# State-space products split between VectorE and GpSimd, results placed three steps behind

## The chip, the cores and the metric

The kernel runs on one core of a Trainium2 chip. The core has five engines, each with its own queue of instructions, executed in order: TensorE (PE in the profile; PEld is its weight load), VectorE (DVE), ScalarE (ACT), GpSimd (POOL) and SyncE (SP, which here only issues DMAs). The metric is the device time of one execution in microseconds, the median of several runs.

## The reference, cut to what matters

Two small networks run one behind the other on the same activations of 256 tokens and 1024 features, all in float32. The first has two layers, each with a token mixer and a feed-forward part with a short convolution. The second has two layers too; its first mixer contains a state-space part (S5) with complex diagonal states. Before that part can run, its parameters have to be discretised:

```python
dt = exp(log_dt); mag = exp(a_re * dt)
abar_re, abar_im = mag * cos(a_im * dt), mag * sin(a_im * dt)
coef_re = (xr * ar + xi * ai) / den;  coef_im = (xi * ar - xr * ai) / den   # xr = abar_re - 1, xi = abar_im
bb_re = coef_re * br - coef_im * bi
bb_im = coef_re * bi + coef_im * br
...
s[t] = abar * s[t-1] + bb @ u[t]            # complex, per group and state
y = s_re @ c_re.T - s_im @ c_im.T + d * u
```

The kernel handles four tokens at a time. So it needs `bb`, `abar * bb`, `abar^2 * bb`, `abar^3 * bb`, and likewise `c` times `abar` to the powers one to four: eight complex products in two chains of four.

## The kernel before, in words

Activations lie with features on the 128 partitions and tokens along the free dimension. Every weight matrix is streamed from memory in pieces of 1024 columns (`Piece`). Each piece is split into a high and a low part so that three fast matmuls replace one float32 matmul: ACT casts the high part (`whi`, L170), DVE subtracts it to get the low part (`wlo`, L172), and PE runs the three matmuls of `mm3` (L187, L188, L189). Four buffers each hold raw pieces, high parts and low parts.

A feed-forward part (`ffn`) has 22 chunks. Each chunk is two pieces, 16 groups of three matmuls, and then a tail: DVE scales the result (`ag`, L526), ACT and DVE do the convolution (`cv`, L531 and twice L539), ACT applies the activation (L541), POOL multiplies by the gate (`cv`, L542), ACT casts the high part (`ah`, L543), and POOL subtracts for the low part (`al`, L544).

The S5 preparation is a generator, `S5.prepare`. It runs as `side` work in the feed-forward part of the last layer of the first network: after each chunk, one or two `next(side)` trace a further stretch of it. `tc.issue_after` orders the POOL instructions of such a stretch behind that chunk's `al` on POOL, and orders nothing on other engines. A `yield` ends a stretch; each half (real or imaginary) of a complex product is one stretch.

A half is three POOL instructions on 128x256 elements (L728, L729, L730), with `tm` as scratch, whose tag differs for the two halves. The result is passed to `place`, which keeps a list `late`. When the list is longer than one, the oldest result is placed: two ACT activations (L721) copy it, masked by `half`, into the two 16-column sides of the padded matrices `B`, `C` or `C0` (the profile calls them s5b, s5c and E). The products alternate between two buffers in `pk` (s5pk), and read both halves of the product before. Sixteen halves follow one another: four products for `B` in one chain, four for `C` in another, in the same two buffers. Behind them stand small matmuls (L757), an ACT copy (L760), 32 transposes (L767) with ACT copies (L768), and the table of rotations (`turn`) on POOL.

The order of instructions on each engine is not the program's. The kernel is built with an automatic scheduler that orders the instructions of each queue by simulated times, with the program's order as priority, and inserts the waits. Inside one queue nothing can overtake at run time.

Of the kernel before, what the change touches and what calls it, by code (L numbers as in the profile page):

```python
# [14 lines left out]
ALU = mybir.AluOpType  # L15
# [83 lines left out]
def build(tc, A, O, stop=None):  # L99
    nc = tc.nc  # L100
    es = ExitStack()
    pool = lambda **k: es.enter_context(tc.tile_pool(**k))
    with es:
# [530 lines left out]
        class S5:  # L634
# [23 lines left out]
            def prepare(self, lbp):  # L658
# [6 lines left out]
                G2, GS = nc.gpsimd.tensor_tensor, nc.gpsimd.tensor_scalar  # L665
# [43 lines left out]
                x = lambda c: c.unsqueeze(2).to_broadcast([128, 16, 16])  # L709
                late = []  # L710

                def place(dst, v):

                    late.append((dst, v))
                    if len(late) > 1:
                        placed()

                def placed():
                    dst, v = late.pop(0)
                    for g in range(2):  # L720
                        nc.scalar.activation(dst[:, :, 16 * g:16 * g + 16], v, AF.Copy, scale=self.half[:, g:g + 1])  # L721

                def times(dst, o, a, re, im, ops=(ALU.subtract, ALU.add)):

                    for c, op in enumerate(ops):
                        tm = sp.tile([128, 512], F32, tag="t%d" % c, name="tm", bufs=1)[:, :256] \
                            .rearrange("p (a b) -> p a b", a=16)
                        G2(o[c], a[c], x(re), op=ALU.mult)  # L728
                        G2(tm, a[1 - c], x(im), op=ALU.mult)  # L729
                        G2(o[c], o[c], tm, op=op)  # L730
                        place(dst[c], o[c])
                        yield

                two_ = lambda t: [t[:, 0], t[:, 1]]
                b = [[B[:, c, :, j, :] for c in range(2)] for j in range(4)]
                at, to = two_(pk[:, 0]), two_(pk[:, 1])
                yield from times(b[3], to, at, cr, ci)
                for j in (2, 1, 0):
                    at, to = to, at
                    yield from times(b[j], to, at, are, aim)  # L740
                at, to = two_(Cp), two_(pk[:, 1])
                for c in range(2):
                    place(C0[:, c], at[c])
                for j in range(4):
                    yield from times(two_(C[:, j]), to, at, are, aim, (ALU.add, ALU.subtract))
                    at, to = to, (two_(pk[:, 0]) if j == 0 else at)
# [567 lines left out]
```

## Time and profile before

| what | value |
|---|---|
| median of 3 runs | 1554.58 us (1554.15 to 1555.01) |
| the profiled execution's own time | 1554.38 us |
| its span, first to last instruction | 1552.4 us |
| PE busy | 1516.7 us, 98% of the span |
| DVE, ACT, POOL busy | 1049.8, 794.9, 585.8 us |
| mean granted clock of PE | 0.992 |

The span lies inside the execution's own time; 2 us of start and end are around it. PE's busy time comes from modelled ends of pipelined matmuls, so its share tells less than the number of matmuls in a stretch of known length. The granted clock is a share of full speed.

### The profile page before, as it was taken

Reading aid. Unit: us, or ns where it says so; the run is one execution under the profiler, and the core shown is the slowest. Engines: PE = TensorE matmul, PEld = TensorE weight load, DVE = VectorE, ACT = ScalarE, POOL = GpSimd, SP = SyncE. Lnnn points to the kernel's source line nnn. Section 1 sums busy time; section 2 is a strip of 40 time slices with the busy share of each in tenths; the row PEclk is TensorE's granted clock in tenths of the full one; section 3 lists DMA queues with packets and bytes.
Section 4 is the critical chain, followed back from the end, with each engine's and each line's share of the span. In section 5 each row is a group of like instructions: output and inputs, shape, how many; then the busy total and the mean of one; then the engine's idle time right before and its main releaser. Section 6 shows DMA issues by size and latency. Waiting matters only on the chain.

```text
span 1552.4 us, 31045 instructions
## 1 busy us (share of the span) xinstructions
PE 1516.7 (98%) x12596; PEld 1479.0 (95%) x12596; DVE 1049.8 (68%) x1384; ACT 794.9 (51%) x1228; POOL 585.8 (38%) x610
## 2 busy tenths in 40 slices
PE   9999999999999999999989999999999998999997
PEld 8899999999999999999988999999999997999997
DVE  6856566877666666657567587888676667677654
ACT  4644444555444544445565644456555446565542
POOL 6500023433326000124998694435333312333332
PEclk9999999999999999999999999999999999999998
DMA  8554355555465644565444464335554554355553
GB/s 260 186 183 148 122 179 189 190 178 182 150 207 169 213 167 136 145 198 179 159 136 150 136 191 165 122 110 197 187 181 155 181 170 140 109 191 183 168 166 109
DMA packets 86574, 259.55 MB, mean 167 GB/s; under 512 B 13592, under 2 KB 24744, under 8 KB 86432
## 3 DMA queue, kind: packets, MB, share of 16 engines
q1 hardware_dynamic: 78688, 254.05, 50.5%
q10 hardware_dynamic: 7584, 3.21, 0.8%
q8 instruction: 98, 1.61, 0.4%
q0 software_dynamic: 160, 0.32, 0.1%
q14 instruction: 44, 0.36, 0.1%
HBM read 255.92 MB, written 1.10 MB: 166 GB/s over the span
## 4 chain that ended last, share of the span: by engine, by line
PE 80%; POOL 8%; DVE 7%; issue 2%; ACT 2%; DMA 1%; DVEq 0%; ACTq 0%; POOLq 0%
PE ps_mm L187 25%; PE ps_mm L188 25%; PE ps_mm L189 25%; DVE wlo L172 3%; POOL s5pk L730 1%; DVE xl L247 1%; POOL al L544 1%; PE ps_sm L443 1%; POOL tm L729 1%; POOL s5pk L728 1%; ACT whi L170 1%; DVE h L474 1%; PE ps_mm L1108 1%; POOL sq L259 0%; POOL cv L542 0%
## 5 line engine op out<-in xcount | busy, mean ns | idle before, releaser
L172 DVE TENSOR_TENSOR wlo<-raw,whi 128x1024 fp32r<-128x1024 f32 (+3 forms) x536 | 638.1, 1205 | 279.8 <-ACT whi L170 270.8
L170 ACT CAST whi<-raw 128x1024 fp32r<-128x1024 f32 (+3 forms) x536 | 510.2, 957 | 428.6 <-PE ps_mm L188 352.9
L189 PE MATMUL ps_mm<-xh,wlo 128*128 128x256 f32 x2352 | 670.8, 285 | 9.4 <-DVE wlo L172 9.2
L187 PE MATMUL ps_mm<-xh,whi 128*128 128x256 f32 x2352 | 669.4, 285 | 3.7 <-ACT whi L170 1.9
L188 PE MATMUL ps_mm<-xl,whi 128*128 128x256 f32 x2352 | 669.6, 285 | 1.7 <-DVE xl L247 1.7
L189 PEld LDWEIGHTS ps_mm<-xh,wlo 128*128 128x128 f32 x2352 | 453.1, 193 | 12.7 <-DVE wlo L172 12.7
L187 PEld LDWEIGHTS ps_mm<-xh,whi 128*128 128x128 f32 x2352 | 453.3, 193 | 5.2 <-ACT whi L170 4.9
L188 PEld LDWEIGHTS ps_mm<-xl,whi 128*128 128x128 f32 x2352 | 453.1, 193 | 4.3 <-DVE xl L247 4.2
L187 PE MATMUL ps_mm<-ah,whi 128*128 128x256 f32 x704 | 199.4, 283 | 0.0
L189 PE MATMUL ps_mm<-ah,wlo 128*128 128x256 f32 x704 | 199.3, 283 | 0.0
L188 PE MATMUL ps_mm<-al,whi 128*128 128x256 f32 x704 | 199.3, 283 | 0.0
L542 POOL TENSOR_TENSOR cv<-cv,ag 128x256 f32<-128x256 f32 x88 | 109.2, 1241 | 222.4 <-ACT cv L541 202.0
L259 POOL TENSOR_TENSOR sq<-h 128x256 f32<-128x256 f32 (+1 forms) x47 | 68.2, 1450 | 179.2 <-DVE h L567 88.0
L188 PEld LDWEIGHTS ps_mm<-al,whi 128*128 128x128 f32 x704 | 135.2, 192 | 0.0
L189 PEld LDWEIGHTS ps_mm<-ah,wlo 128*128 128x128 f32 x704 | 135.2, 192 | 0.0
L187 PEld LDWEIGHTS ps_mm<-ah,whi 128*128 128x128 f32 x704 | 135.2, 192 | 0.0
L539 DVE SCALAR_TENSOR_TENSOR cv<-ag,vec,cv 128x255 f32<-128x255 f32 (+1 forms) x176 | 95.9, 545 | 17.2 <-ACT cv L531 14.2
L465 POOL TENSOR_TENSOR gate<-gate 128x256 f32<-128x256 f32 x16 | 19.4, 1225 | 203.1 <-DVE gate L464 203.1
L544 POOL TENSOR_TENSOR al<-cv,ah 128x256 fp32r<-128x256 f32 x88 | 73.8, 838 | 45.8 <-ACT ah L543 45.8
L543 ACT CAST ah<-cv 128x256 fp32r<-128x256 f32 x88 | 35.7, 406 | 103.1 <-POOL cv L542 103.1
L526 DVE TENSOR_TENSOR ag<-ps_mm,rb 128x512 f32<-128x512 f32 x88 | 60.4, 687 | 38.5 <-PE ps_mm L189 38.1
L262 POOL TENSOR_TENSOR acc<-acc,sq 128x256 f32<-128x256 f32 x57 | 58.2, 1022 | 3.9
(343 smaller groups left out, 2120.4 us busy)
## 6 DMA issues: line engine op xcount, KB each, us to landing
raw<-w_up SPq DMA_DIRECT2D x88, 512.0 KB, 3.7
raw<-w_fi SPq DMA_DIRECT2D x88, 512.0 KB, 4.0
raw<-w_qk SPq DMA_DIRECT2D x48, 512.0 KB, 3.7
raw<-w_gate SPq DMA_DIRECT2D x32, 512.0 KB, 3.6
raw<-w_down SPq DMA_DIRECT2D x32, 512.0 KB, 3.6
raw<-w_fo SPq DMA_DIRECT2D x32, 512.0 KB, 3.6
raw<-w_v SPq DMA_DIRECT2D x24, 512.0 KB, 4.3
raw<-w_u SPq DMA_DIRECT2D x16, 512.0 KB, 6.2
```

Source lines behind the costliest of these rows:

```text
L170: nc.scalar.copy(self.hi[:, :n], raw[:, :n])
L172: eng.tensor_tensor(self.lo[:, :n], raw[:, :n], self.hi[:, :n].bitcast(F32), op=ALU.subtract)
L187: nc.tensor.matmul(out, lhsT=a[0], rhs=b[0], start=start, stop=False)
L188: nc.tensor.matmul(out, lhsT=a[0], rhs=b[1], start=False, stop=False)
L189: nc.tensor.matmul(out, lhsT=a[1], rhs=b[0], start=False, stop=stop)
L259: nc.gpsimd.tensor_tensor(q, hs, hs, op=ALU.mult)
L262: nc.gpsimd.tensor_tensor(acc, acc if k0 + i > 1 or n == 1 else q[:, 0, :], q[:, i, :], op=ALU.add)
L526: nc.vector.tensor_tensor(ag, ps, bc2(rb), op=ALU.mult)
L539: nc.vector.scalar_tensor_tensor(out=c[:, o], in0=a[:, s_], scalar=w[j], in1=c[:, o], op0=ALU.mult, op1=ALU.add)
L542: nc.gpsimd.tensor_tensor(c, c, ag[:, 1, :], op=ALU.mult)
L543: nc.scalar.copy(ah[:, i, :], c)
L544: last = nc.gpsimd.tensor_tensor(al[:, i, :], c, ah[:, i, :].bitcast(F32), op=ALU.subtract)
```

## The change

`G2`, which was `nc.gpsimd.tensor_tensor`, is replaced in `times` by an engine that goes with the half: the real half (c = 0) runs on VectorE, the imaginary half (c = 1) stays on GpSimd. All three instructions of a half go to one engine. The list of results waiting to be placed may now hold three.

```diff
                     late.append((dst, v))
-                    if len(late) > 1:
+                    if len(late) > 3:
                         placed()
...
                     for c, op in enumerate(ops):
                         tm = sp.tile([128, 512], F32, tag="t%d" % c, name="tm", bufs=1)[:, :256] \
                             .rearrange("p (a b) -> p a b", a=16)
-                        G2(o[c], a[c], x(re), op=ALU.mult)
-                        G2(tm, a[1 - c], x(im), op=ALU.mult)
-                        G2(o[c], o[c], tm, op=op)
+                        G = (nc.vector, nc.gpsimd)[c].tensor_tensor
+                        G(o[c], a[c], x(re), op=ALU.mult)
+                        G(tm, a[1 - c], x(im), op=ALU.mult)
+                        G(o[c], o[c], tm, op=op)
                         place(dst[c], o[c])
                         yield
```

`placed` and everything before and behind the products are unchanged. What remains in the list at the end is placed by the `while late` loop, as before.

## Rows read from the trace of the kernel before

**Rows 1.** The page: busy time by engine, and the last chain by line.
```profile
PE 1516.7 (98%) x12596; PEld 1479.0 (95%) x12596; DVE 1049.8 (68%) x1384; ACT 794.9 (51%) x1228; POOL 585.8 (38%) x610
...
PE ps_mm L187 25%; PE ps_mm L188 25%; PE ps_mm L189 25%; DVE wlo L172 3%; POOL s5pk L730 1%; DVE xl L247 1%; POOL al L544 1%; PE ps_sm L443 1%; POOL tm L729 1%; POOL s5pk L728 1%; ACT whi L170 1%; DVE h L474 1%; PE ps_mm L1108 1%; POOL sq L259 0%; POOL cv L542 0%
```

**Rows 2.** Stretches: length, busy PE, PEld, DVE, ACT, POOL, clock, DMA share, GB/s.
```profile
680.00:700.00 20.00, 20.00 (x169) 20.00 (x168) 10.85 (x12) 8.93 (x12) 5.91 (x5) 1.00 0.63 197
780.09:853.87 73.78, 65.10 (x610) 61.68 (x609) 50.24 (x50) 44.00 (x80) 65.82 (x70) 0.98 0.43 144
853.87:865.00 11.13, 8.81 (x62) 8.54 (x61) 6.42 (x9) 8.35 (x15) 3.62 (x5) 0.85 0.34 109
```

**Rows 3.** Groups by line, from 780.09 to 853.87 us: busy, mean, idle before.
```profile
L187 PE MATMUL ps_mm<-xh,whi 128*128 128x256 f32 x158 | 45.8, 290 | 1.9 <-ACT whi L170 1.9
```

**Rows 4.** Waits of PE, ACT, DVE, POOL, 780 to 860: total us, times, longest.
```profile
PE ps_mm L189 <- DVE wlo L172: 6.5, 8, 1.3
PE ps_aux L767 <- ACT s5k L760: 2.3, 1, 2.3
...
ACT s5c L721 <- POOL s5pk L730: 12.5, 7, 2.3
ACT s5b L721 <- POOL s5pk L730: 6.7, 5, 2.0
...
DVE wlo L172 <- ACT whi L170: 18.7, 10, 3.2
...
POOL al L544 <- ACT ah L543: 8.9, 8, 1.7
```

**Rows 5.** Chain that ended last, within one chunk: start us, us, what.
```profile
834.69 1.47 POOL al L544
...
837.76 1.61 POOL s5pk L730
...
839.40 0.72 ACT s5c L721 x2
...
840.23 0.38 ACT ah L543
```

**Rows 6.** Timeline of the same chunk, DVE then POOL: start us, us, instruction.
```profile
834.34 1.23 DVE L172 TENSOR_TENSOR wlo<-raw,whi 128x1024 fp32r<-128x1024 f32 x1 [1.91 <-ACT whi L170]
...
837.13 1.64 DVE L172 TENSOR_TENSOR wlo<-raw,whi 128x1024 fp32r<-128x1024 f32 x1
838.69 0.68 DVE L526 TENSOR_TENSOR ag<-ps_mm,rb 128x512 f32<-128x512 f32 x1
...
836.88 0.80 POOL L729 TENSOR_TENSOR tm<-s5pk,s5p 128x256 f32<-128x256 f32 x1
837.76 1.60 POOL L730 TENSOR_TENSOR s5pk<-s5pk,tm 128x256 f32<-128x256 f32 x1
```

**Rows 7.** Lines: ns min/median/max, first and last start; L172 within 780 to 860.
```profile
L728 POOL TENSOR_TENSOR s5pk<-s5pk,s5p x14: 613/802/1607, 780.1 to 850.6; 128x256 f32<-128x256 f32 x14
L730 POOL TENSOR_TENSOR s5pk<-s5pk,tm x16: 727/1597/1760, 784.5 to 852.3; 128x256 f32<-128x256 f32 x16
L820 DVE TENSOR_TENSOR w<-w x4: 409/416/420, 965.4 to 1014.9; 128x256 f32<-128x256 f32 x4
L172 DVE TENSOR_TENSOR wlo<-raw,whi x21: 1207/1622/1741, 780.8 to 855.8; 128x1024 fp32r<-128x1024 f32 x21
L539 DVE SCALAR_TENSOR_TENSOR cv<-ag,vec,cv x176: 470/484/961, 287.8 to 1479.6; 128x255 f32<-128x255 f32 x132, 128x254 f32<-128x254 f32 x44
L542 POOL TENSOR_TENSOR cv<-cv,ag x88: 726/1458/1700, 291.4 to 1481.8; 128x256 f32<-128x256 f32 x88
L544 POOL TENSOR_TENSOR al<-cv,ah x88: 723/743/1493, 292.7 to 1483.8; 128x256 fp32r<-128x256 f32 x88
```

**Rows 8.** Timeline of ACT, then POOL, at the first products.
```profile
786.98 0.91 ACT L721 ACTIVATE s5b<-s5pk,s5h 128x256 f32<-128x256 f32 x2
...
789.84 1.72 POOL L730 TENSOR_TENSOR s5pk<-s5pk,tm 128x256 f32<-128x256 f32 x1
```

## The prediction

> **What bounds the kernel now.** I read the busy shares first: TensorE (PE) is busy for 1516.7 of 1552.4 us, and by line the chain that ended last is nearly all matmul [rows 1]. So almost every stage is set by PE, and in such a stage a faster VectorE (DVE) or GpSimd (POOL) gives nothing. Then I asked which stage is not. The products of the change (L728 to L730) run only from 780.09 to 853.87 us. The table by stretch [rows 2] compares this with a stretch of the same layer in which PE never stops: 169 matmuls in 20 us, or 20/169 = 0.118 us each. In the products' stretch 158 of the L187 matmuls began [rows 3]; L188 and L189 have as many, so 474 matmuls, which need 474 x 0.118 = 56.1 us, and with some 3 us for the small matmuls of L757 and L767 the need is 59.2 us. It took 73.8. So about 14.6 us are lost here, and 1.5 of them are the granted clock (0.98 in the mean). The 11 us behind it hold another 3.4: 62 matmuls where the full pace gives 94, less the slots that eight transposes take, at a clock of 0.85 [rows 2].
>
> Then the waits in this stretch [rows 4]. PE waits for the low parts of the weight pieces (wlo of L172, 6.5 us) and once, for 2.3 us, for the ScalarE (ACT) copy of L760. Those are symptoms. DVE waits 18.7 us for ACT's casts, ACT waits 12.5 + 6.7 = 19.2 us for POOL's L730 before it places a result (L721), and POOL waits 8.9 us for ACT's `ah`. POOL is busy for 65.8 of 73.8 us [rows 2]. The chain of waits over one chunk says the same: al, the three product instructions, two placings, ah, and the next al [rows 5]. So the bound of this stretch is a loop through POOL, with ACT's placing in it.
>
> The timeline shows a second thing [rows 6]. POOL and DVE instructions that both read two SBUF operands stretch each other: wlo takes 1.23 us, and 1.64 where it begins while POOL's L729 runs; L730 takes 1.60 beside it, against 0.73 at its shortest [rows 7]; L526, whose first operand lies in PSUM, keeps its 0.68. They take turns: wlo began at 837.13, L729 ended at 837.68, and wlo ended 1.09 us after that.
>
> **The change, part by part.** *Moved work.* Sixteen halves (eight products, real and imaginary) of three POOL instructions each become eight on POOL and eight on DVE, so 24 instructions move. A half on POOL costs, at the shortest durations, 0.61 + 0.61 + 0.73 = 1.95 us (L729 is of L728's form and length); the nearest DVE row is a tensor_tensor of the same 128x256 with both operands in SBUF, L820, at 0.416, so 3 x 0.42 = 1.25 us [rows 7]. If the two engines ran side by side, POOL would be rid of half of its products and the whole 14.6 us could come back. But they take turns, so I add up what the two must do one after another. Per chunk of the feed-forward layer: two wlo at 1.21, two L539 at 0.47, cv 0.73, al 0.72, in all 4.81 us [rows 7]. The stretch has 158/16 = 9.9 chunks: 47.6 us, and with 16 x 1.95 = 31.2 it is 78.8 us, against the 73.8 that it took (ends and starts of neighbours overlap by some hundredths each), a ratio of 0.937. With the change it is 47.6 + 8 x 1.95 + 8 x 1.25 = 73.2, times 0.937 = 68.6 us. That is still over PE's 59.2, so the pair stays the bound and the difference counts in full: **5.2 us** saved. Below, it could be nothing (if the loop through ACT alone sets the pace); above, 14.6.
>
> The Trainium skill ("SBUF — State Buffer", section "Who interferes with whom") says that a VectorE instruction with two SBUF inputs contends with a GpSimd instruction that reads SBUF, that the shared port pair is an exclusive lock, and that the one which comes second blocks fully. The trace agrees, with 1.23 against 1.64 us above. It speaks against reading the move as relief of POOL: by that page only 5.2 us are to be had, and without the lock 14.6.
>
> *Placing three behind.* The number of L721 activations stays 32. What is released later in the program need not stand later in the queue: ACT placed a result at 786.98 though by the program its turn comes only when the next result has been formed, whose L730 began at 789.84 [rows 8]. The tool that orders the instructions had pulled it forward. So I don't count on ACT's 19.2 us of waits disappearing. But half of the results now come from DVE and POOL has less queued, so placings wait less, `ah` comes sooner, and POOL waits less for it. The bound is POOL's 8.9 us for `ah` above and zero below; I take **2 us**, near the lower end for the reason just given.
>
> *New waits.* A real half on DVE reads the imaginary result of the product before, and overwrites what that product read, so DVE now waits for POOL, up to seven times, and everything behind it in DVE's queue waits as well: wlo, for which PE already waits, then L539 and L526. The trace of before has no such wait in this stretch; the nearest is ACT's wait for the same L730, 19.2/12 = 1.6 us each [rows 4]. So the cost lies between 0 and 7 x 1.6 = 11.2 us. Mostly POOL is executing the half meanwhile, and DVE's two-input work couldn't run beside that anyway; and DVE idles 18.7 us here already. I take **1 us** lost. The first instruction of a half also waits until ACT has placed the result that lay in its buffer, four results before. That is two products back, and ACT is busy for 44.0 of 73.8 us [rows 2]; zero, and if that cover goes, it falls under the same 11.2.
>
> *Behind the products.* L760 stands behind the last placing on ACT, so the gap of 2.3 us and the slow clock after it (3.4 us in all) hang on when the last half is done. That half is imaginary, stays on POOL, and is queued behind the last chunks' al. But the half ahead of it leaves POOL's queue. Between 0 and 3.4; I take half, **1.7 us**.
>
> Sum: 5.2 + 2 + 1.7 - 1 = **7.9 us**. Against the profiled execution's own 1554.38 this gives 1546.5; its span would go from 1552.4 to 1544.5. That execution lies 0.2 us under the median of the three runs, which is nothing here, and I state **1546.5**.
>
> **Rivals.** (1) *The whole loss comes back.* If the pieces of weights held ahead let PE run through the turns of the pair, 14.6 + 3.4 = 18 us return: 1536.4. For it: PE waits only some 9 us directly [rows 4], so a small lead would do. Against it: 73.2 us of work for the pair in a stretch where PE needs 59.2. (2) *Slower: DVE becomes the place where the loop is closed.* DVE's queue order is fixed, and if each real half stands where POOL's result is expected but not yet there, wlo is held behind it. With the full 11.2, only the 5.2 for the pair, and nothing for placing or tail, the time is 1554.4 - 5.2 + 11.2 = 1560.4. For it: ACT met just this wait in 12 of 16 placings, and DVE feeds PE more directly than ACT's placings did. Against it: POOL would have less queued ahead of the half. It decides from 5.2 + 3.1 = 8.3 us in all, 1.2 us for each of seven waits; less gives no change. (3) *The change doesn't do what it says.* Work leaves POOL, but al still waits for ah, ah for the placing, and the placing for a half: the same loop with another engine in it. Then the 5.2 us are eaten by seven waits of 0.74 us each and the time stays at 1554. For it: the order shown in rows 8. Against it: in chunks with a real half POOL has only cv and al.
>
> By the Trainium skill ("GPSIMD Engine Reference", section "Engine selection") two-input element-wise work belongs on VectorE, GpSimd being about twice as slow. The rows here show 0.61 to 0.73 against 0.42 us, a factor of 1.5 to 1.8; with a factor of two, a DVE half would cost 0.98 and the sum would be 2 us better.
>
> **How the numbers follow.** About 0.2%, 3.1 us, is what a measurement can tell from no change. Forecast 0.56 (1541 to 1551), everything back 0.10 (near 1536), no change 0.19 (the third rival, or the second with waits near 1 us), slower 0.15 (1558 to 1561). So faster 0.66, same 0.19, slower 0.15. The range runs from 1538.5 to 1560: it leaves out most of the first rival and the far end of the second, some 0.14 together; inside it lie the bounds of the unknown terms taken one at a time.
>
> **What would show it.** In the changed profile, the stretch of the products should take about 66 to 69 us where it took 73.8, with POOL busy for some 50 us; DVE's products should take 0.42 us alone and up to a us beside POOL. ACT's waits for L730 should fall by half, and DVE should show waits for L730 of POOL of a few us in total. If those exceed 8 us, rival 2 holds. If PE's matmuls fill the stretch, I was wrong to keep the pair as the bound. If the order of matmuls elsewhere changes and the difference lies outside 780 to 865 us, the whole argument missed.

## The result and the profile after

The changed kernel takes 1546.22 us in the median of 4 runs (1545.66 to 1547.49), the kernel before 1554.6. The ratio is 0.9945, with a 95% interval of 0.9932 to 0.9957: 8.4 us faster. The forecast was 1546.5 us.

The place is the one that the argument named. The stretches of the changed kernel that answer to [rows 2] are these: a full-speed stretch of the same layer, the products' stretch from the first to the last product, and the 11.13 us behind it (columns as in [rows 2]; the lines of the products have moved by one and are L729 to L731 now).

```profile
680.00:700.00 20.00, 20.00 (x169) 20.00 (x168) 11.20 (x13) 8.84 (x12) 4.78 (x5) 1.00 0.61 193
780.88:847.70 66.82, 61.74 (x610) 59.79 (x610) 62.21 (x76) 45.03 (x82) 46.22 (x46) 1.00 0.48 161
847.70:858.83 11.13, 9.70 (x82) 9.44 (x82) 6.40 (x8) 8.36 (x15) 3.64 (x4) 1.00 0.35 110
```

PE did as much work, 610 matmuls, in 66.82 us instead of 73.78: 7.0 us. Behind it 82 matmuls began where 62 did, which at 0.118 us each is 2.4 us more. The two gains make 9.4 us. About 8 us are still lost in the stretch. POOL is busy for 46.2 us (65.8 before) and DVE for 62.2 (50.2 before), nearly the whole stretch. The profiled execution is the slowest of the four, 1547.49 us, and had lost 1.7 us before the products began, so the median is the better number for the whole and the stretch for the place.

The waits from 780 to 860 us (total us, times, longest), PE, ACT, DVE, then POOL, answer to [rows 4]:

```profile
PE ps_mm L189 <- DVE wlo L172: 4.9, 6, 1.7
PE ps_aux L768 <- ACT s5k L761: 1.4, 1, 1.4
...
ACT s5c L721 <- POOL s5pk L731: 5.7, 4, 1.7
ACT s5b L721 <- POOL s5pk L731: 1.9, 2, 1.1
ACT s5b L721 <- DVE s5pk L731: 1.6, 2, 1.0
...
ACT s5c L721 <- DVE s5pk L731: 0.9, 1, 0.9
...
DVE wlo L172 <- ACT whi L170: 7.7, 5, 2.8
DVE s5pk L729 <- POOL s5p L702: 1.2, 1, 1.2
DVE s5pk L729 <- POOL tm L730: 1.0, 2, 0.5
...
POOL cv L542 <- ACT cv L541: 18.6, 9, 4.6
POOL al L544 <- ACT ah L543: 9.5, 11, 2.1
```

PE still waits for wlo. ACT's waits for a product fell from 19.2 to 10.1 us. DVE's new waits for POOL are three, 2.2 us in all, and one of them is the start of the chain. POOL now mostly waits for the chunk's own work. The chain that ended last has changed in part. From 804 us (start us, us, what) it runs through DVE's queue, where [rows 5] was a loop through POOL:

```profile
804.21 0.74 DVE s5pk L731
804.95 1.56 DVE wlo L172
806.51 0.76 DVE tm L730
807.27 0.88 DVE cv L539
808.15 0.33 DVE s5pk L729
```

Later it still runs as in [rows 5]: from 816.50 us al, then a half's three instructions on POOL, then the placings on ACT from 820.30. So the loop has not gone from the stretch; it sets the pace in fewer places.

And the lines of the products (ns min/median/max), to be read beside [rows 7]:

```profile
L731 DVE TENSOR_TENSOR s5pk<-s5pk,tm x8: 410/790/952, 783.6 to 841.2; 128x256 f32<-128x256 f32 x8
L731 POOL TENSOR_TENSOR s5pk<-s5pk,tm x8: 801/864/1604, 784.2 to 846.1; 128x256 f32<-128x256 f32 x8
```

Alone a product takes 0.41 us on DVE; its median of 0.79 is with POOL at work beside it.

### The profile page after: what moved, and what is told of

Its sections match the earlier page's. It is cut to its first block, busy times and chain, and to the rows that moved or that the text cites. A ratio compares the mean times of both kernels' runs of the same rounds, so it can differ in the third digit from the quotient of the medians.

```text
span 1545.3 us, 31040 instructions
## 1 busy us (share of the span) xinstructions
PE 1511.9 (98%) x12596; PEld 1475.3 (95%) x12596; DVE 1058.2 (68%) x1408; ACT 794.9 (51%) x1228; POOL 564.6 (37%) x586
## 4 chain that ended last, share of the span: by engine, by line
PE 77%; POOL 9%; DVE 9%; issue 3%; ACT 2%; DMA 0%; DVEq 0%; ACTq 0%; POOLq 0%
PE ps_mm L187 24%; PE ps_mm L188 24%; PE ps_mm L189 24%; DVE wlo L172 3%; DVE xl L247 1%; ACT whi L170 1%; POOL sq L259 1%; PE ps_sm L443 1%; POOL acc L262 1%; POOL hg L587 1%; POOL al L544 1%; POOL cv L542 1%; DVE h L474 1%; PE ps_mm L1109 1%; PE ps_sm L275 0%
## 5 line engine op out<-in xcount | busy, mean ns | idle before, releaser
L172 DVE TENSOR_TENSOR wlo<-raw,whi 128x1024 fp32r<-128x1024 f32 (+3 forms) x536 | 634.8, 1199 | 266.9 <-ACT whi L170 256.8
L189 PE MATMUL ps_mm<-xh,wlo 128*128 128x256 f32 x2352 | 669.4, 285 | 7.8 <-DVE wlo L172 7.5
L187 PE MATMUL ps_mm<-xh,whi 128*128 128x256 f32 x2352 | 667.9, 284 | 2.3 <-DVE gate L464 1.8
L189 PEld LDWEIGHTS ps_mm<-xh,wlo 128*128 128x128 f32 x2352 | 452.0, 192 | 10.3 <-DVE wlo L172 10.2
L187 PEld LDWEIGHTS ps_mm<-xh,whi 128*128 128x128 f32 x2352 | 452.2, 192 | 3.0 <-ACT whi L170 2.8
L542 POOL TENSOR_TENSOR cv<-cv,ag 128x256 f32<-128x256 f32 x88 | 115.7, 1315 | 235.3 <-ACT cv L541 214.8
L187 PE MATMUL ps_mm<-ah,whi 128*128 128x256 f32 x704 | 199.3, 283 | 0.0
L189 PE MATMUL ps_mm<-ah,wlo 128*128 128x256 f32 x704 | 199.2, 283 | 0.0
L187 PEld LDWEIGHTS ps_mm<-ah,whi 128*128 128x128 f32 x704 | 135.2, 192 | 0.0
L189 PEld LDWEIGHTS ps_mm<-ah,wlo 128*128 128x128 f32 x704 | 135.2, 192 | 0.0
L539 DVE SCALAR_TENSOR_TENSOR cv<-ag,vec,cv 128x255 f32<-128x255 f32 (+1 forms) x176 | 93.9, 534 | 10.4 <-ACT cv L531 7.5
L262 POOL TENSOR_TENSOR acc<-acc,sq 128x256 f32<-128x256 f32 x57 | 60.3, 1058 | 3.9
```

The costliest lines, as they stand in the source:

```text
L172: eng.tensor_tensor(self.lo[:, :n], raw[:, :n], self.hi[:, :n].bitcast(F32), op=ALU.subtract)
L187: nc.tensor.matmul(out, lhsT=a[0], rhs=b[0], start=start, stop=False)
L189: nc.tensor.matmul(out, lhsT=a[1], rhs=b[0], start=False, stop=stop)
L262: nc.gpsimd.tensor_tensor(acc, acc if k0 + i > 1 or n == 1 else q[:, 0, :], q[:, i, :], op=ALU.add)
L539: nc.vector.scalar_tensor_tensor(out=c[:, o], in0=a[:, s_], scalar=w[j], in1=c[:, o], op0=ALU.mult, op1=ALU.add)
L542: nc.gpsimd.tensor_tensor(c, c, ag[:, 1, :], op=ALU.mult)
```

## The experiments

The theory to be tested: two-input work of DVE and POOL takes turns, and the sum of both engines' work sets the pace of the stretch until it falls under what PE needs ("turns" in the expectations). Its rivals: the loop through ACT's placing sets the pace ("loop"), or DVE's queue by itself does ("queue").

**Each part of the change alone.** Two kernels, one with the split and the old list, one with the old engines and the longer list.

```diff
-                    if len(late) > 3:
+                    if len(late) > 1:          # e1: changed kernel, split alone
```
```diff
-                    if len(late) > 1:
+                    if len(late) > 3:          # e2: kernel before, placing later alone
```

> The changed kernel with the list of results waiting to be placed back at one: the engine split alone. The scheduler pulled placings forward in the kernel before, and here the queues of all engines, waits included, come out as in the changed kernel. So the split alone gives everything: 1546 us, within 2 us. If placing later had a share, 1548 or above.

> The kernel before with the list at three: placing later alone. The queues come out as in the kernel before, so no change: 1554.5 us, within 2 us. If placing later had a share, 1552 or under.

Measured: the split alone 1546.59 us, ratio 0.9938 (0.9923 to 0.9954); placing later alone 1555.43 us, ratio 0.9996 (0.9987 to 1.0004). The split is the change. Laid side by side, the queues of all engines hold the same instructions in the same order: e1's as the changed kernel's, e2's as those of the kernel before. So the later place in the program changed nothing that the scheduler decided.

The two pairs also show what the place itself varies by. I take the time between the same two matmuls of L187, those that begin at 770.7 and 880.4 us in the kernel before, in the profile of each run: 109.7 us before and 108.2 in e2; 100.3 in the changed kernel and 99.8 in e1. With equal queues it differs by up to 1.5 us. This measure is used again below as "the place".

**The other half to DVE as well.**

```diff
-                        G = (nc.vector, nc.gpsimd)[c].tensor_tensor
+                        G = nc.vector.tensor_tensor
```

> The imaginary halves go to VectorE too, so no product runs on GpSimd. Turns theory (two-input work of VectorE and GpSimd excludes each other, and its sum sets the pace of the stretch): the sum falls once more by 8 x (1.95 - 1.25) x 0.937 = 5.2 us, to 63.4 us against the 59.2 that TensorE needs, so about 1541 us. Loop theory (the loop al, half, placing, ah, al through ScalarE sets the pace): the half leaves GpSimd's queue wholly, so al no longer stands behind a half, and the time falls to near 1537. Queue theory (VectorE's own queue is what is short now): VectorE gets 8 x 1.25 = 10 us more and the time rises, to 1550 or above.

Measured: 1541.44 us, ratio 0.9906 (0.9888 to 0.9924). That is near the number of the turns theory, and far from the queue theory's 1550. From the loop theory's 1537 it is not far: the interval of the ratio reaches from 1537.6 to 1543.2 us, and the profiled execution took 1539.1. In the place the second step brought 4.4 us (95.9 against 100.3) of the 5.2 expected. Stretches (columns as in [rows 2]) and the products' line:

```profile
780.00:800.00 20.00, 17.83 (x146) 17.45 (x145) 19.80 (x35) 14.67 (x26) 8.18 (x5) 1.00 0.48 157
800.00:820.00 20.00, 18.83 (x155) 18.42 (x154) 20.00 (x35) 15.68 (x29) 7.87 (x8) 1.00 0.52 170
...
L731 DVE TENSOR_TENSOR s5pk<-s5pk,tm x16: 408/412/948, 782.1 to 829.8; 128x256 f32<-128x256 f32 x16
```

With POOL busy for only 8 of 20 us, a product on DVE has a median of 0.41 us instead of 0.79. DVE is full, 19.8 to 20 of 20 us, and yet the time fell: a full queue of DVE costs less here than the same work split over two engines that exclude each other. PE still starts only 146 and 155 of 169 matmuls.

**Extra work for DVE, with two operands and with one.** In the changed kernel, three extra DVE instructions per real half on the same 128x256 operand, their results unused. `scr` is the unused half of the scratch tile of `tm`.

```diff
                         G(o[c], o[c], tm, op=op)
+                        if c == 0:
+                            for _ in range(3):
+                                nc.vector.tensor_tensor(scr, a[c], x(re), op=ALU.mult)                    # e7
+                                nc.vector.tensor_reduce(scr[:, :, 0], a[c], axis=AX.X, op=ALU.max)        # e8, instead
                         place(dst[c], o[c])
```

> The changed kernel with three extra VectorE products per real half (24 in all, 128x256, both operands in SBUF, result unused). Turns theory: they take turns with GpSimd as the moved ones do, so the sum of both rises by 24 x 0.42 x 0.937 = 9.4 us and the time goes from 1546 to 1551 to 1556 us. Queue theory (only VectorE's own queue counts, GpSimd runs beside it): the same rise, but then the same in the twin kernel with one input. No-bound theory (neither counts, idle time takes them): 1546 to 1548.

> The twin: 24 extra VectorE instructions of the same 128x256 read, but a reduction with one operand in SBUF. Turns theory: they occupy VectorE for the same 0.42 us, but GpSimd runs beside them, so GpSimd's products and al are not stretched by them; the time stays at least 3 us under the twin with two inputs, 1546 to 1551. Queue theory: the same time as the twin, within 2 us.

Measured on the same chip: 1552.41 us with two operands (ratio 0.9986, 0.9977 to 0.9995), 1548.2 with one (0.9955, 0.9942 to 0.9967). The extra instructions' line, L734 in both, first e7, then e8:

```profile
L734 DVE TENSOR_TENSOR tm<-s5pk,s5p x21: 409/821/965, 780.0 to 843.3; 128x256 f32<-128x256 f32 x21
```
```profile
L734 DVE TENSOR_REDUCE tm<-s5pk x21: 404/409/417, 652.0 to 836.1; 128x16 f32<-128x256 f32 x21
```

The two are equally long when nothing is in the way, 0.41 us. With two operands the median is double; with one, no instance exceeds 0.417 us, whatever POOL did. The same work on DVE therefore costs 4.2 us more when it excludes POOL; in the place 3.4 of it is seen (106.3 against 102.8 us). The queue theory, which wanted equal times, falls. The pair isn't perfect: a reduction writes 16 elements where a product writes 256, and three of the 24 reductions needed nothing but a loaded matrix and ran at 652 to 659 us; at 0.41 us each those are 1.2 us.

**ScalarE's placing taken out of the loop.** The placings copy the matrix that came by DMA, so they wait for no product. The products are still formed, but not placed.

```diff
-  nc.scalar.activation(dst[:, :, 16 * g:16 * g + 16], v, AF.Copy, scale=self.half[:, g:g + 1])
+  nc.scalar.activation(dst[:, :, 16 * g:16 * g + 16], Cp[:, 0], AF.Copy, scale=self.half[:, g:g + 1])   # e5: in before, e6: in after
```

> The kernel before, all products on GpSimd, but the placings copy the matrix that came by DMA instead of the product's result: the 32 activations stay, and ScalarE waits for no product, nor a product for a placing. Numerically another result. Turns theory: the work of the two engines is unchanged (78.8 x 0.937 = 73.8 us), so 1551 to 1554 us. Loop theory: the loop is cut, and most of the 14.6 us comes back, 1545 us or less.

> The changed kernel with the same cut: the placings copy the matrix that came by DMA, so ScalarE waits for no product. Turns theory: the sum of the two engines' work stays 68.6 us, so 1543 to 1546 us. Loop theory: what is left of the loop goes, 1538 to 1541.

Measured: e5 1559.73 us, ratio 1.0028 (1.0017 to 1.0040), e6 1554.87, ratio 0.9996 (0.9985 to 1.0007). Both theories missed the totals, and as totals these are failures of design. Free of their waits, all 32 placings of products were ordered to where the matrix had arrived, 129 us and more before their old places, one behind the other; from e5:

```profile
656.00:678.00 22.00, 19.88 (x163) 19.26 (x162) 9.76 (x11) 21.62 (x48) 3.65 (x5) 0.92 0.45 145
```

ACT is full there, PE starts 163 matmuls where the kernel before started 186 in the same 22 us, and the granted clock fell to 0.92. What can be read is the products' stretch, first e5, then e6:

```profile
790.00:860.30 70.30, 62.15 (x518) 59.16 (x517) 49.62 (x49) 31.73 (x50) 63.81 (x69) 1.00 0.46 150
```
```profile
788.70:855.70 67.00, 62.28 (x510) 59.58 (x509) 58.08 (x74) 32.49 (x51) 44.62 (x45) 0.97 0.47 154
```

The first line stops short of the last product, which ends at 861.1 us, so e5's stretch is 71.1 us. The stretches don't hold the same work: some 100 of the small matmuls have moved out of e5's and e6's. So I compare each with what PE needs for the matmuls that began in it, 0.118 us for each of L187 to L189 and, from the distances of their starts, 2.8 us for the small ones in the two kernels with all of them, 1.5 us in e5 and 0.7 us in e6. Over this need 15.1 us are lost in the kernel before and 12.7 in e5, 8.1 in the changed kernel and 10.2 in e6. Taking ACT out of the loop is worth about 2.4 us in the kernel before, not far above what equal queues differ by, and nothing that can be seen in the changed one. The loop theory, which wanted most of 14.6 us back, falls, though by a reading of stretches and not by the totals. Since the move also freed 12 us of ACT within the stretch, the 2.4 us are not the loop's alone.

**The floor.** First the products were left out and the placings copied the matrix that came by DMA.

```diff
-                        G(o[c], a[c], x(re), op=ALU.mult)
-                        G(tm, a[1 - c], x(im), op=ALU.mult)
-                        G(o[c], o[c], tm, op=op)
-                        place(dst[c], o[c])
+                        place(dst[c], Cp[:, c])
```

> Leaves out all 48 product instructions; the 32 placings stay and copy the matrix that came by DMA, so they wait for no product. This is the floor: what the products cost in all, on any engine. Turns theory and loop theory alike: near 1536 us, 18 us under the kernel before (14.6 in the stretch, 3.4 behind it). If the time stays above 1545, the loss in that stretch doesn't come from the products, and both theories fall.

Measured: 1543.53 us, ratio 0.9922 (0.9906 to 0.9939), which is neither number. The placings were again pulled forward, to places between 656 and 782 us, and cost their own stall there (columns as in [rows 2]):

```profile
760.00:780.00 20.00, 16.07 (x131) 15.31 (x129) 8.39 (x12) 12.05 (x27) 15.52 (x31) 0.91 0.33 106
780.00:800.00 20.00, 20.00 (x169) 19.46 (x169) 14.46 (x17) 18.76 (x28) 10.10 (x20) 0.92 0.57 182
800.00:820.00 20.00, 20.00 (x169) 20.00 (x168) 15.60 (x21) 12.14 (x20) 8.11 (x8) 1.00 0.62 191
```

From 780 us PE starts 169 of 169, so the loss in the products' stretch goes with the products; the total isn't the floor. The next kernel keeps everything in its place: the kernel before, with each product cut to 16 of its 256 elements (the rest of the result isn't computed; a `memset` fills the second buffer once).

```diff
+                        f = lambda t: t[:, :, 0:1]
-                        G2(o[c], a[c], x(re), op=ALU.mult)
+                        G2(f(o[c]), f(a[c]), f(x(re)), op=ALU.mult)      # and the other two likewise
```

> The kernel before with the 48 GpSimd products cut from 256 elements to 16 per partition (the rest of the result is not computed), so the chain of products, placings, ah and al is the same in kind, but each product takes about 0.22 us as the small GpSimd instructions of the preparation do. Turns theory: the sum of both engines falls by 16 x (1.95 - 0.66) = 20.6 us, under what TensorE needs, so everything comes back: 1536 to 1540. Loop theory: the same loop with its links shorter by 1.3 us a half, but ScalarE's placing still in it: 1540 to 1545.

Measured: 1537.74 us, ratio 0.9889 (0.9876 to 0.9903). The chain of products, placings, ah and al is the same in kind, ACT still places behind every product, and 17 us came back, 15.1 of them in the place (94.6 us). So it was the products' length on POOL, not the loop's existence: the loop theory wanted 1540 or more. Alone this run can't tell turns from a loop with shorter links; e7 and e8 do that.

**Pacing.** With all products on DVE nothing tied a half to its chunk, as `issue_after` ties POOL's. Here each DVE half is queued behind the chunk's convolution, first with all products on DVE (e10), then in the changed kernel (e11).

```diff
-                    with tc.issue_after(last.ins):
+                    with tc.issue_after(last.ins), tc.issue_after(conv.ins):     # conv: the chunk's last L539
```

> All products on VectorE, and each half is queued behind the convolution of its chunk on VectorE (L539), as GpSimd's were behind al. With all products on VectorE and unpaced, VectorE was busy 19.8 of 20 us from 780 to 840 us and TensorE still lost some 4 us from 780 to 820. If bunching is what is left, pacing gives up to 4 us more: 1538 to 1540 us. If VectorE is simply full there, no change: 1541 to 1542.

> The changed kernel (real half on VectorE, imaginary on GpSimd) with VectorE's halves queued behind the convolution of their chunk, as in the paced kernel with all products on VectorE. Turns theory: the sum of both engines' work, 68.6 us, is still over the 59.2 that TensorE needs, so pacing can't give what it gave there: 1543 to 1547. If bunching alone was what cost the changed kernel its time, near 1539.

Measured: e10 1538.53 us, ratio 0.9892 (0.9877 to 0.9907); e11 1545.1, ratio 0.9926 (0.9912 to 0.9940). e10 is the fastest version found, 16.3 us under the kernel before, 0.8 us over the kernel whose products are cut. Its own stretches:

```profile
780.00:800.00 20.00, 19.19 (x147) 19.19 (x148) 20.00 (x34) 14.96 (x27) 7.85 (x6) 0.91 0.50 163
800.00:820.00 20.00, 20.00 (x169) 20.00 (x168) 20.00 (x33) 15.59 (x28) 11.77 (x8) 1.00 0.54 181
```

From 800 us PE runs at full pace beside a full DVE; what e10 still loses here, it loses in the first 20 us, where PE starts 147 of 169 matmuls. The sum of the turns theory, 63.4 us, is over PE's 59.2 for this kernel too, so it marks where the pair stops being the bound only roughly. Pacing isn't shown to be worth anything: the intervals of e3 and e10 overlap, as do e11's and the changed kernel's, and in the place pacing changed 95.9 to 95.4 us and 100.3 to 100.3. That it can't rescue the split is shown: e10 and e11 differ only in the engine of the imaginary half, by 6.6 us in the medians and 5.3 by the ratios, each to the kernel before on the same chip, and these intervals lie apart.

## Why the prediction was right, point by point

*The bound.* I put the loss at 14.6 us in the stretch and 3.4 behind it, 18 in all. e9 gives 17.0 back, 15.1 of them in the place. That PE wasn't the bound there holds. That the bound was a loop through POOL with ACT's placing in it holds for the part of POOL's work; ACT's placing had at most some 2.4 us of it (e5).

*Moved work, 5.2 us, and the rule of turns.* This carries the prediction, and the runs bear it out where it could fail: e7 and e8 separate two operands from one, and e3 made a second such step, 4.4 us in the place where 5.2 were expected. That its median of 1541.4 us fell on the expected 1541 is in part luck, since its five runs lie between 1539.1 and 1542.3. The Trainium skill ("SBUF — State Buffer", section "Who interferes with whom") lists tensor_reduce as an instruction that never contends on this chip; the trace agrees, with 0.404 to 0.417 us against 0.409 to 0.965.

*The size of that term, and placing, 2 us.* Here the sum was better than its parts. Added up from all instructions of both traces, DVE's instructions with two SBUF operands (wlo, L539 and the products) or POOL's were under way for 67.8 of 73.8 us before and for 63.6 of 66.8 after. So the work of the two shrank by about 4.3 us, not 5.2, and the gaps in which neither ran by about 2.7 us, where placing less new waits was to give 1. The step that failed is the reason for the 2 us: POOL's waits for ah didn't fall (8.9 us before, 9.5 after). Why the gaps shrank is open. That the total came out within 0.3 us is therefore luck in part: the terms were off by up to 1.7 us either way.

*Placing three behind.* I took the queue's order to be the scheduler's and counted on nothing from it. e1 and e2 show exactly that.

*New waits, 1 us.* Measured 1.0 us in two waits until POOL's L730 had read what the half overwrites, plus 1.2 us once at the start, where the preparation's last numbers come from POOL. That start costs more at first: DVE's queue has the first two products ahead of a wlo that began at 777.93 us before and now begins at 781.99. PE takes 13.3 us there for the matmuls that took it from 775 to 785 us before; by 800 us the loss of 3.4 us was made good. The far end, 11.2 us, didn't come: no wait of DVE for POOL's result (L731) shows at all. That this is because POOL has less queued is likely, not shown.

*Behind the products, 1.7 us.* Measured 2.4. PE's gap at the transposes is 1.4 us instead of 2.3, and the granted clock is 1.00 there instead of 0.85.

*The sum.* 7.9 us forecast, 8.4 by the medians, 9.4 in and just behind the stretch of the profiled execution. A part of that is lost again: at the first L567 behind the products the profile is 7.7 us ahead of before (881.15 against 888.83 us), at L187's matmul that begins at 964 us before only 5.8, at the end 7.1. In between PE waits 1.6 us for a POOL sum (acc, L262), a wait that the profile of before doesn't show there. e2's profile has it too, with the queues of the kernel before, and e3, e8 and e10 don't, so it comes and goes and isn't the split's.

*The rivals.* Everything back: not by this change, which still loses 8.1 us in the stretch with POOL busy for only 46.2 of 66.8; but by e10 nearly so. Slower: no. The same loop with another engine in it: the chain still shows it in places, but seven new waits of 0.74 us didn't come, and the gain stayed. The list did nothing, as e2 shows.

## What to carry to other kernels

Before moving element-wise work from GpSimd to VectorE to relieve it, add up the work of both engines with two operands in SBUF as if they were one, at their durations when alone. What the move gains is then about the difference of the two durations, not the time taken off the busier engine: here 4.3 us of shared work, where POOL's busy time fell by 19.6. Where the sum is still over what TensorE needs, try moving the rest too; here a full VectorE beside a GpSimd busy for 8 of 20 us was better than a balanced pair. And when a scheduler orders the queues, compare the queues before pricing an edit that only moves a line in the program.

## What the hardware did unexpectedly

Turns between the two engines are not fair. In e7 POOL's `cv` (0.73 us at its shortest) took 3.08 us (timeline: start us, us, instruction; POOL first, then DVE):

```profile
792.28 3.08 POOL L542 TENSOR_TENSOR cv<-cv,ag 128x256 f32<-128x256 f32 x1 [5.27 <-ACT cv L541]
...
792.54 1.21 DVE L172 TENSOR_TENSOR wlo<-raw,whi 128x1024 fp32r<-128x1024 f32 x1
793.68 0.41 DVE L729 TENSOR_TENSOR s5pk<-s5pk,s5p 128x256 f32<-128x256 f32 x1
794.02 0.41 DVE L730 TENSOR_TENSOR tm<-s5pk,s5p 128x256 f32<-128x256 f32 x1
794.35 0.41 DVE L734 TENSOR_TENSOR tm<-s5pk,s5p 128x256 f32<-128x256 f32 x1
794.69 0.95 DVE L539 SCALAR_TENSOR_TENSOR cv<-ag,vec,cv 128x255 f32<-128x255 f32 x1
```

Four DVE instructions with two SBUF operands followed one another, each at its full speed, while POOL's instruction, begun before them, ended 0.6 us behind the last of them; only the fifth, L539, was stretched, from 0.47 to 0.95 us. Nor had I expected what placings without a wait can cost by being ordered early, which is the scheduler's doing: from 640 to 700 us the profile of e5 fell 7.7 us behind that of the kernel before, and e6's 7.1.
